# Gradient along rows: loads that wait for their slot's store only, and a second store in two pieces

## The chip, the cores and the metric

The kernel runs on one core of a Trainium2 chip. The metric is the time of one execution on the device, in microseconds (us); lower is better. A core has several engines with their own instruction streams. Three of them matter here: VectorE (DVE in the profile), which does the arithmetic; GpSimd (POOL), which does a little of it; and SyncE (SP), whose stream mostly issues transfers. ScalarE's stream (ACT) issues transfers too. Transfers between the main memory (HBM) and the on-chip memory (SBUF) run on sixteen DMA engines of the core. SP and ACT each have a queue of transfers on all sixteen; in the profile SP's is q1 and ACT's is q10.

## The reference

```python
def setup_inputs():
    return {"x": np.random.randn(8192, 8192).astype(np.float32)}

def reference(x):
    return np.gradient(x, axis=1)
```

Along each row, an inner element of the result is half the difference of its right and left neighbours: out[j] = (x[j+1] - x[j-1]) / 2. The first is x[1] - x[0], the last x[8191] - x[8190], both without the half. Input and output have 268.4 MB each, so 536.9 MB have to be moved.

## The kernel before, in words

The 8192 rows are cut into 32 tiles (`nsets`) of 256 rows. A tile gives each of the 128 partitions two neighbouring rows (`R = 2`), which lie side by side in HBM: 16,384 numbers, 64 KB a partition, 8.39 MB a tile. SBUF holds three slots (`NB = 3`) that the tiles use in turn. A slot is 64 numbers longer than a tile (`SH`): a tile is loaded 64 columns to the right, and its result is written from column 0, over the input that was already used. So a slot holds a tile from its load to the end of its store, and the load of tile i + 3 needs the store of tile i to be complete.

The order of the work is written out by hand (`manual_schedule`), and each instruction is told which earlier step it waits for (`chain`, L45 to L56; `keep` is the list of steps that it waits for). For tile i:

- SP issues the load (`load`, L60).
- GpSimd computes the four end differences of the two rows into `ends` (L72), as soon as the load has landed.
- VectorE computes the halved differences over both rows at once, 16,382 columns (L83). It also writes the two rows' ends wrongly, since it runs across the border between them.
- The right ends are copied over from `ends` (L94), by VectorE, or by GpSimd for tiles with i % 5 equal to 1 or 3.
- The store is issued (L97): by ACT for tiles 0 to 29, by SP for tiles 30 and 31.
- The load of tile i + 3 is issued by SP (L103, L60).

Tile 31 goes through L83, L94 and L97 twice, a row at a time, so the kernel has 33 stores; in this text stores 0 to 30 are those of tiles 0 to 30. Loads 0, 1 and 2 are issued at once at the start and stand behind each other in SP's queue.

From load 3 on a load waits for two things before it is issued: the store of tile i - 3 (L63), and the load in front of it, which must have landed (L62, `loads[-1]`, given the reason "queue empty"). SP works through its stream in order, so SP's queue never holds two loads after the first three.

Of the kernel before, what the change touches and what calls it, by code (L numbers as in the profile page):

```python
# [1 line left out]

# [4 lines left out]


@with_exitstack
def kernel(  # L10
    ctx: ExitStack,
    tc: tile.TileContext,
    x: bass.AP,
    out: bass.AP,
):

    nc = tc.nc
    P = nc.NUM_PARTITIONS
    n, m = x.shape
    R = 2
    NB = 3
    SH = 64  # L30
    W = R * m
    nsets = n // (P * R)
    f32 = x.dtype

    x_sets = x.rearrange("(s p t) m -> s p (t m)", p=P, t=R)
    out_sets = out.rearrange("(s p t) m -> s p (t m)", p=P, t=R)

    pool = ctx.enter_context(tc.tile_pool(name="pool", bufs=1))
    slots = [pool.tile([P, SH + W], f32, name=f"slot{k}", tag=f"slot{k}") for k in range(NB)]
    ends = pool.tile([P, nsets, R, 2], f32, name="ends", tag="ends")  # L40
    landed = mybir.DependencyInfo(mybir.DependencyClass.Sync, mybir.DependencyReason.DATA)
    loads, stores = [], [None] * nsets
    in_front = {}

    def chain(i, ins, *needed):  # L45

        group, engine = f"slot{i % NB}", ins.ins.engine
        keep = [o.ins for o in needed]  # L50
        if in_front.get(engine, (None,))[0] == group:
            keep.append(in_front[engine][1])
        tc.declare_no_dep(ins.ins, group=group, keep=keep, reason="implied by the needed step")
        tc.add_to_no_dep_group(group, ins.ins)
        in_front[engine] = group, ins.ins
        return ins  # L56

    def load(i):
        b = slots[i % NB]
        ins = nc.sync.dma_start(out=b[:, SH : SH + W], in_=x_sets[i])  # L60
        if i >= NB:
            tc.add_manual_dep(ins.ins, loads[-1].ins.name, landed, reason="queue empty")  # L62
        loads.append(chain(i, ins, *([stores[i - NB]] if i >= NB else [])))  # L63

    with tc.manual_schedule():
        for i in range(NB):
            load(i)
        for i in range(nsets):
            b = slots[i % NB]
            xin = b[:, SH : SH + W].rearrange("p (t m) -> p t m", m=m)  # L70

            ins = nc.gpsimd.tensor_sub(  # L72
                out=ends[:, i, :, :],
                in0=xin[:, :, 1 : m : m - 2],
                in1=xin[:, :, 0 : m - 1 : m - 2],
            )
            at = [chain(i, ins, loads[i])]
            last = i == nsets - 1
            nr = 1 if last else R
            for r in range(0, R, nr):  # L80
                c0, c1 = r * m + 1, (r + nr) * m - 1

                ins = nc.vector._custom_dve(  # L83
                    dve_ops.TENSOR_TENSOR_REDUCE_SUB_MAX,
                    out=b[:, c0:c1],
                    in0=b[:, SH + c0 + 1 : SH + c1 + 1],
                    in1=b[:, SH + c0 - 1 : SH + c1 - 1],
                    s0=0.0,
                    s1=0.5,
                )  # L90
                halved = chain(i, ins, *at)
                res = b[:, r * m : (r + nr) * m].rearrange("p (t m) -> p t m", m=m)
                placer = nc.gpsimd if i % 5 in (1, 3) and not last else nc.vector
                ins = placer.tensor_copy(out=res[:, :, 0 : m : m - 1], in_=ends[:, i, r : r + nr, :])  # L94
                placed = chain(i, ins, halved)
                queue = nc.scalar if i < nsets - 2 else nc.sync
                ins = queue.dma_start(  # L97
                    out=out_sets[i, :, r * m : (r + nr) * m], in_=b[:, r * m : (r + nr) * m]
                )
                stores[i] = chain(i, ins, placed)  # L100
                at = [halved]
            if i + NB < nsets:
                load(i + NB)  # L103


# [1 line left out]
_INS = ['x']  # L107
_OUTS = [((8192, 8192), 'float32')]


# [23 lines left out]
```

## Time and profile before

| | |
|---|---|
| time, median of 4 runs | 1248.5 us (1247.49 to 1319.02) |
| the profiled execution's time, its span | 1248.07 us, 1246.2 us |
| VectorE | 554.8 us busy, 45% of the span |
| GpSimd | 8.8 us busy |
| L83 over two rows | 17.22 us each, 31 times |
| issue of a load, of a store on ACT | 0.33 us, 0.34 us |
| a load, from issue to landing | 38.6 us (median) |
| a store on ACT, from issue to landing | 37.9 us (median) |

The four runs are 1248.07, 1248.93, 1247.49 and 1319.02 us. The span is the time from the first to the last instruction of the profiled execution. A row of the profile's groups names line, engine, operation and shape, then how often it ran, its busy time and the mean of one in ns, and the engine's idle time before it with what ended it. The chain is the sequence of steps that ended last, each followed back to what released it. In the DMA issues, "to landing" is the time from the issuing instruction to the completion of the transfer, so it includes the time that the transfer stood in its queue.

### The profile page before, as it was taken

The page shows a single profiled execution, that of the slowest core. Times are in us where ns is not written, and L with a number is a line of the kernel's source. Part 1 is how long each engine was busy: PE and PEld are TensorE (multiplying, and loading weights), DVE is VectorE, ACT ScalarE, POOL GpSimd, SP SyncE. Part 2 cuts the span into 40 slices and gives each one's busy share as a digit, 9 for nine tenths or more (in the row PEclk, how much of TensorE's full clock was granted, in tenths as well). Part 3 has the DMA queues.
Part 4 walks back from the last instruction along what each step waited for, and adds up shares of the span by engine and source line. Part 5 has one row for each costly group of instructions (what it writes and reads, how often), then busy time and mean ns, then how long its engine had stood idle before and what let it go on. Part 6 is the DMA issues. An engine that isn't in the chain of part 4 may idle for free.

```text
span 1246.2 us, 267 instructions
## 1 busy us (share of the span) xinstructions
DVE 554.8 (45%) x54; POOL 8.8 (1%) x48
## 2 busy tenths in 40 slices
DVE  2841453345533455334554245543355433554363
POOL 0000000000000000000000000000000000000000
DMA  9999999999999999999999999999999999999998
GB/s 404 438 438 438 423 429 427 435 433 438 438 435 438 438 429 431 427 433 433 435 438 433 435 438 412 433 431 433 431 433 438 431 417 431 438 438 433 438 438 374
DMA packets 9360, 536.88 MB, mean 431 GB/s; under 512 B 1040, under 2 KB 1040, under 8 KB 1040
## 3 DMA queue, kind: packets, MB, share of 16 engines
q1 hardware_dynamic: 5040, 285.21, 53.2%
q10 hardware_dynamic: 4320, 251.66, 46.6%
HBM read 268.44 MB, written 268.44 MB: 431 GB/s over the span
## 4 chain that ended last, share of the span: by engine, by line
DMA 93%; DVE 3%; issue 2%; SPq 0%; POOL 0%; POOLq 0%
DMA slot<-in_x_dram 90%; DMA out_dram<-slot 3%; DVE slot L83 3%; DVE slot L94 0%; SPq L60 0%; POOL ends L72 0%; POOLq L129 0%
## 5 line engine op out<-in xcount | busy, mean ns | idle before, releaser
L83 DVE CUSTOM_DVE_ANT_0 slot<-slot 128x16382 f32<-128x16382 f32 (+1 forms) x33 | 551.3, 16706 | 669.0 <-POOL ends L72 669.0
L72 POOL TENSOR_TENSOR ends<-slot 128x4 f32<-128x4 f32 x32 | 6.3, 198 | 989.9 <-DMA slot<-in_x_dram 989.9
L94 DVE COPY slot<-ends 128x4 f32<-128x4 f32 (+1 forms) x21 | 3.6, 171 | 0.7
L94 POOL COPY slot<-ends 128x4 f32<-128x4 f32 x12 | 2.3, 190 | 207.9 <-DVE slot L83 207.9
L118 POOL MEMSET const-uint8-127<- 128x1 uint8 x1 | 0.1, 102 | 0.0
L118 POOL MEMSET const-bfloat16-1.0<- 128x1 bf16 x1 | 0.1, 101 | 0.0
L118 POOL MEMSET const-float32-0.0<- 128x1 f32 x1 | 0.1, 98 | 0.2 <-issue 0.2
L118 POOL MEMSET const-float32-1.0<- 128x1 f32 x1 | 0.1, 99 | 0.0
## 6 DMA issues: line engine op xcount, KB each, us to landing
out_dram<-slot SPq DMA_DIRECT2D x2, 4096.0 KB, 20.3
slot<-in_x_dram SPq DMA_DIRECT2D x32, 38.6
out_dram<-slot ACTq DMA_DIRECT2D x30, 37.9
out_dram<-slot SPq DMA_DIRECT2D x1, 30.8
```

The lines of the kernel that those rows point to most:

```text
L72: ins = nc.gpsimd.tensor_sub(out=ends[:, i, :, :], in0=xin[:, :, 1 : m : m - 2], in1=xin[:, :, 0 : m - 1 : m - 2],)
L83: ins = nc.vector._custom_dve(dve_ops.TENSOR_TENSOR_REDUCE_SUB_MAX, out=b[:, c0:c1], in0=b[:, SH + c0 + 1 : SH + c1 + 1], in1=b[:, SH + c0 ...
L94: ins = placer.tensor_copy(out=res[:, :, 0 : m : m - 1], in_=ends[:, i, r : r + nr, :])
L118: nc = _bacc.Bacc("TRN2", target_bir_lowering=False, num_devices=1)
```

## The change

The load loses its wait for the load in front (L41 and L62 go). It waits for the stores of its slot alone, so a load may be issued while the one in front still runs, and then stands behind it in SP's queue. The list of stores of a tile becomes a list of lists, so that a load waits for each piece of the store. The store of tile 1 is issued as two transfers, one behind the other on ACT: the first 896 columns of the 16,384 (3,584 B a partition, 0.46 MB in all), and the other 15,488 (61,952 B a partition).

```diff
     W = R * m
+    FIRST = 896
     nsets = n // (P * R)
...
-    landed = mybir.DependencyInfo(mybir.DependencyClass.Sync, mybir.DependencyReason.DATA)
-    loads, stores = [], [None] * nsets
+    loads, stores = [], [[] for _ in range(nsets)]
...
         ins = nc.sync.dma_start(out=b[:, SH : SH + W], in_=x_sets[i])
-        if i >= NB:
-            tc.add_manual_dep(ins.ins, loads[-1].ins.name, landed, reason="queue empty")
-        loads.append(chain(i, ins, *([stores[i - NB]] if i >= NB else [])))
+        loads.append(chain(i, ins, *(stores[i - NB] if i >= NB else [])))
...
                 queue = nc.scalar if i < nsets - 2 else nc.sync
-                ins = queue.dma_start(
-                    out=out_sets[i, :, r * m : (r + nr) * m], in_=b[:, r * m : (r + nr) * m]
-                )
-                stores[i] = chain(i, ins, placed)
+                c0, c1 = r * m, (r + nr) * m
+                cuts = [c0, c0 + FIRST, c1] if i == 1 else [c0, c1]
+                for a0, a1 in zip(cuts, cuts[1:]):
+                    ins = queue.dma_start(out=out_sets[i, :, a0:a1], in_=b[:, a0:a1])
+                    stores[i].append(chain(i, ins, placed))
                 at = [halved]
```

## The prediction

> **What bounds the kernel now.** I read the page first (which engine is full), then the chain (what ends last), then the DMA queue's waits and issues, and last the times at which single tiles land.
>
> ```profile
> span 1246.2 us, 267 instructions
> DVE 554.8 (45%) x54; POOL 8.8 (1%) x48
> DMA packets 9360, 536.88 MB, mean 431 GB/s; under 512 B 1040, under 2 KB 1040, under 8 KB 1040
> q1 hardware_dynamic: 5040, 285.21, 53.2%
> q10 hardware_dynamic: 4320, 251.66, 46.6%
> DMA slot<-in_x_dram 90%; DMA out_dram<-slot 3%; DVE slot L83 3%; DVE slot L94 0%; SPq L60 0%; POOL ends L72 0%; POOLq L129 0%
> ```
>
> The queue rows give packet time as a share of sixteen DMA engines: 53.2% + 46.6% = 99.8%. The transfer engines are full from end to end; VectorE at 45% is not the bound. So removing a wait can't remove idle time. It can only alter how fast full engines work.
>
> ```profile
> 22.75 0.20 POOL L72 TENSOR_TENSOR ends<-slot 128x4 f32<-128x4 f32 x1 [22.31 <-DMA slot<-in_x_dram]
> 42.07 0.20 POOL L72 TENSOR_TENSOR ends<-slot 128x4 f32<-128x4 f32 x1 [19.12 <-DMA slot<-in_x_dram]
> 22.68:42.00 19.32, 17.39 (x2) 0.20 (x1) 1.00 1.00 434
> ```
>
> The timeline's first two rows are L72 starting as tiles 0 and 1 land; no store has begun, so the difference, 19.32 us, is what 8.39 MB costs alone, 434 GB/s in the windows' last column. All 64 tile-sized transfers at that rate take 64 x 19.32 = 1236.5 us. Before them lie 0.74 us to the first issue and 22.68 - 0.74 - 19.32 = 2.6 us until data flow; after the last landing (1245.31) 0.9 us. That makes 1240.7 us. The span has 5.5 us more: the whole of what can be won, 0.44%.
>
> ```profile
> SPq L60 <- DMA slot<-in_x_dram: 1162.0, 29, 77.0
> SPq L60 <- DMA out_dram<-slot: 2.4, 1, 2.4
> slot<-in_x_dram SPq DMA_DIRECT2D x32, 38.6
> out_dram<-slot ACTq DMA_DIRECT2D x30, 37.9
> ...
> 81.48 41.04 DMA slot<-in_x_dram
> 122.58 44.20 DMA slot<-in_x_dram
> 247.24 38.68 DMA slot<-in_x_dram
> 672.38 39.17 DMA slot<-in_x_dram
> 1021.67 39.71 DMA slot<-in_x_dram
> 1138.76 38.66 DMA slot<-in_x_dram
> ```
>
> SP's own waits: only load 3 was released by a store, all others by the load in front. The chain's rows (start, us) are loads end to end, each beside a store at half rate: 38.6 where two lone transfers would take 38.64. From 247.24 to 1177.48 (the 25 landings of tiles 6 to 30) the mean step is 930.24 / 24 = 38.76 us, 0.12 over the floor.
>
> **Where the 5.5 us sit.** The trace also holds every DMA packet. By start and end they fall into sixteen gapless rows, one per engine: 512 packets' worth each, one 64 KB packet 2.418 us, a 32 KB packet 1.213. Some packets are longer, nearly all of them loads. Per engine the excess is 0.7 us at the start and 0.8 us at 43.5 us (store 0 comes up), then 3.5 us on the mean engine and 5.0 on the slowest, which ends the kernel. Of the slowest's 5.0, 0.9 follow a load's issue by less than 8.2 us and 2.9 a store's issue; 1.0 fits neither. Those issues found their queue empty or nearly so. Where a transfer was queued well ahead (stores 1, 2 and 3, issued at 59.8, 96.8 and 140.3), the six microseconds after the issue show no long packet.
>
> **Part 1, the wait goes.** It removes 29 semaphore waits from SP and adds none; nothing is issued more often. Ahead of whom do loads move? On SP they stand in program order, stores 30 and 31 behind load 31, so no order changes there. ACT and POOL see nothing of it. How much earlier: in the steady part a store's issue follows the landing of its tile by 0.2 + 0.05 + 17.2 + 0.2 = 17.7 us and lands 37.9 later, at 55.6; two steps of 38.66 make 77.3; so the wait that is removed ends 21.7 us after its slot is free. But that lead grew while loads stalled. At the first place where the change bites, store 1 landed at 117.67 and load 3 at 122.52: load 4 comes 4.85 us earlier. From there both queues hold work, each engine alternates load and store packets, and nothing moves the lead again, so it stays near 5 us. Load 3 was issued at 81.48 and its first packet began at 85.36, 3.9 us later. A lead of 4.85 covers that, by about 1 us, for the engines that run last; for engines that run ahead by up to the 4.6 us spread of landings it doesn't. The last engines alone set the end.
>
> The load's time in the chain doesn't shrink: 38.6 us is two transfers at full rate. What goes is the excess at restarts. Lower end of the gain: 0, if the excess has another origin. Upper end: 5.0 us, all of the slowest engine's excess after 44 us. I take 0.9 + 2.9 = 3.8 us, because stores are then queued 20 us ahead too (store 2, issued 96.8, began about 117) and loads a little ahead, like the rows without excess.
>
> The cover: while load 4's queue stands empty, the store queue works alone. It stays that way in either version, so a late load costs no DMA time. If both queues were empty at once, the price would be the 3.9 us from issue to first packet for each tile; for that a store would have to be late by its 20 us of queueing, and VectorE has 21 us idle before each tile.
>
> **Part 2, store 1 in two pieces.** One more DMA issue on ACT (0.338 us by the row of L97), at 60 us, while store 0 runs to 81.47: hidden by 20 us. On the engines, 8 packets of 3,584 B and 8 of 61,952 replace 8 of 64 KB. The 32 KB packet costs 1.213 us, where half of 2.418 is 1.209: 4 ns per extra packet, 8 x 0.004 + one 9 ns completion packet = 0.04 us. Upper bound: the piece restarts a queue like store 0, 0.8 us. Below nothing: it puts load 3's first packet off by up to a packet and so gives loads more lead; that is at most the gain already counted. I take 0.1 us, near the 32 KB row, because the piece stands behind store 0 and ahead of the rest in a queue with work. The small packets take some 8 x 0.14 = 1.1 us from about 80.5, and load 3's packets come at about 85, so the two hardly meet; the phase shifts by under one packet. Load 4 now waits for two semaphores; both pieces land before load 3 does.
>
> The Trainium skill, "DMA: Bandwidth & Descriptors", section "Bandwidth", speaks against this: it asks for at least 1 MiB per DMA, and lists 0.95 us for 64 KB and 6.15 for 1 MB. The piece has 0.44 MiB; between those rows its estimate is 3.0 us, where its bytes at 434 GB/s are 1.06: by the page the part costs 2.0 us and the sum below would be 1246.3, no measurable change. The table is for transfers issued from GpSimd; no run here shows such a piece yet.
>
> **The tail** stays: 1206.58 to 1245.31 is 38.73 us for the two last tiles' stores, where two transfers need 38.64, with store 30 (30.8 us from issue) covering the last VectorE steps.
>
> **Sum.** The profiled execution took 1248.07 us, 1.9 over its span; the median shown is 1248.5 of four, one of them 70 us off, so I build on 1248.07. 1248.07 - 3.8 + 0.1 = 1244.4 us, 0.3% less. About 0.2%, 2.5 us, is what a measurement here can tell from no change.
>
> **Rivals.**
> *No change (1248).* The long packets belong to the mixing of reads and writes or to memory, not to restarts; or the change doesn't do what it says, since 1 us of spare lead is too thin and loads still find their queue dry. For it: DMA is full in both versions, and loads restarted at 300 to 560 us with hardly an excess (steps 38.64). Against: the clean queued transfers. Gain 0 to 2.5.
> *Slower (1261).* With both queues always full, every load packet runs between store packets; if the 39.17 us step of tile 17 to 18 became the rule, 28 steps would each cost 39.23 - 38.76 = 0.47 us more, +13 us; at the 39.71 us step it would be +28. It decides from 0.09 us per step (2.5 / 28). For it: slow steps exist and cluster (672 to 1061 us), so some alignments of the two streams hurt, and the change fixes an alignment that then never shifts. Against: from 46 to 78 and 86 to 114 us the streams alternated strictly, with every packet at 2.418 but for two, 0.02 and 0.07 us over.
> *Faster (1244.4)*, as summed.
>
> **How the numbers follow.** Faster as summed 0.46, no change 0.33, slower 0.21. The likeliest case's own range is 1242.9 (all 5.0 us, no cost of the piece: 1243.1, less 0.2 for spread of runs) to 1245.6. The overall range must hold no change (1245.6 to 1250.6) and the start of the slower case: 1242 to 1256. Below 1242 there is no room by the floor; what is left out is the upper part of the slower case.
>
> **What would show it.** Right: on SP, L60 waits for out_dram<-slot 28 or 29 times; issue to landing of loads grows from 38.6 to some 43 us, and of stores from 37.9 to some 58 (as store 1 and 2 now); loads still land every 38.64 us; DMA share stays at 99.8% and the span is 3 to 4 us shorter; packets grow by 144. Wrong: landings more than 38.85 us apart (slower); or 38.76 as now (no change). If a slice falls well below 431 GB/s with idle engines, the cover of the two queues failed, and the price is 3.9 us a time.

## The result and the profile after

The changed kernel is slower: median 1250.47 us against 1248.3, ratio 1.0028 with a 95% interval of 1.0018 to 1.0038. Forecast were 1244.4 us and a ratio of 0.997. Its single times lie further apart, from 1245.7 to 1258.0 us over 37 runs; its fastest is 0.5 us from the fastest of before (1245.2). The ratios in this text leave out executions more than 1.5% above the fastest of their kernel: 7 of the 164 of before (1305 to 1342 us), one of e1 (1337) and five of the six of e8 (1336 to 1343), and, between 1264 and 1284 us, three of the six of e9 and one each of e2, e3, e4, e12, e13, e15 and e16.

The page of the changed kernel, the rows that answer to those shown of before:

```profile
span 1250.9 us, 266 instructions
DVE 554.8 (44%) x54; POOL 8.8 (1%) x48
DMA packets 9504, 536.88 MB, mean 429 GB/s; under 512 B 1056, under 2 KB 1056, under 8 KB 1184
q1 hardware_dynamic: 5040, 285.21, 52.8%
q10 hardware_dynamic: 4464, 251.66, 46.4%
```

The two queues' packets take 52.8 + 46.4 = 99.2% of sixteen engines' span, where they took 99.8%. The work is the same; 0.8% of 1250.9 us, 10 us per engine, went unused, against 2.5 us before. The waits of SP and the DMA issues (issue to landing) show the change at work:

```profile
SPq L60 <- DMA out_dram<-slot: 1156.7, 29, 80.1
...
out_dram<-slot ACTq DMA_DIRECT2D x1, 7744.0 KB, 58.8
slot<-in_x_dram SPq DMA_DIRECT2D x32, 43.9
out_dram<-slot ACTq DMA_DIRECT2D x29, 54.9
out_dram<-slot ACTq DMA_DIRECT2D x1, 448.0 KB, 23.4
```

All 29 loads wait for a store now, none for a load. A load takes 43.9 us from issue to landing, that is 38.6 plus a stay of some 5 us in its queue. So the change does what it says. The time went elsewhere. The windows view of the last 19.9 us, before and then after (window, length, VectorE, GpSimd, clock, DMA share, GB/s):

```profile
1226.30:1246.20 19.90, 0.00 (x0) 0.00 (x0) 1.00 0.84 364
```

```profile
1231.00:1250.90 19.90, 0.00 (x0) 0.00 (x0) 1.00 0.52 226
```

At the end of the changed kernel half of the DMA time is empty. Each transfer reports its completion sixteen times, once for each engine; of the last store's sixteen reports, after the first, thirteen lie within 0.12 us, two at 1.3 and 1.4, and one at 8.84 us. In the kernel before fourteen lie within 0.7 us and the last two at 2.0 and 2.1. So one engine is late. An estimate from these reports: without it the profiled execution would have ended 8.84 - 1.42 = 7.4 us earlier, at 1253.08 - 7.4 = 1245.7 us, which is what the fastest runs take. The profiled execution is 2.6 us above the median, and there is no trace of a median one; so that a late engine also makes the 2.2 us between the medians fits, but is not shown.

That engine falls behind slowly. The time between the first and last report of a store grows like this (us):

| store of tile | 5 | 10 | 15 | 20 | 25 | 29 |
|---|---|---|---|---|---|---|
| before | 4.6 | 4.5 | 4.6 | 4.2 | 1.5 | 4.3 |
| after | 3.3 | 6.7 | 7.5 | 11.6 | 13.8 | 17.1 |

(A report comes after the packet of the other queue that is in between, so part of a spread is the turn at which an engine changes queue; the growth is the late engine's.) The long packets tell the same. Over 2.418 us for each 64 KB, the mean engine loses 3.5 us after 44 us in the kernel before and 0.9 after. Followed by start and end, the sixteen rows of before lose 4.4 to 6.7 us in all, startup included; those of after 1.3 to 4.3, and one about 9. Summed up along these rows, the late engine of after has done 1.5 us less work than the median engine at 400 us, 3.4 at 800 and 7.0 at 1200; in before, at steps of 50 us up to 1200, no engine is ever more than 1.9 us behind, and none stays there to the end.

### The profile page after: what moved, and what is told of

The parts are those of the page before. It is cut to its first block, busy times and chain, and to the rows that moved or that the text cites. A ratio compares the mean times of both kernels' runs of the same rounds, so it can differ in the third digit from the quotient of the medians.

```text
span 1250.9 us, 266 instructions
## 1 busy us (share of the span) xinstructions
DVE 554.8 (44%) x54; POOL 8.8 (1%) x48
## 3 DMA queue, kind: packets, MB, share of 16 engines
q1 hardware_dynamic: 5040, 285.21, 52.8%
q10 hardware_dynamic: 4464, 251.66, 46.4%
## 4 chain that ended last, share of the span: by engine, by line
another core or an unknown queue 83%; DMA 9%; issue 3%; DVE 3%; SPq 1%; POOL 0%; POOLq 0%
DMA slot<-in_x_dram 5%; DMA out_dram<-slot 3%; DVE slot L81 3%; SPq L60 1%; DVE slot L92 0%; POOL ends L70 0%; POOLq L131 0%
## 6 DMA issues: line engine op xcount, KB each, us to landing
out_dram<-slot SPq DMA_DIRECT2D x2, 4096.0 KB, 20.3
slot<-in_x_dram SPq DMA_DIRECT2D x32, 43.9
out_dram<-slot ACTq DMA_DIRECT2D x29, 54.9
```

## The experiments

The table comes first, and what each run tells follows. "Excess" is what the mean engine loses in long packets after 44 us, "last" how far the engine that ends last lies behind the one before it; both are of one profiled execution. "Step" is the share of load packets in whose middle fewer than 12 of the other 15 engines load, that is, packets that are out of step with the rest.

| kernel | ratio to before (95%) | excess us | last us | step |
|---|---|---|---|---|
| before | 1 | 3.5 | 0.1 | 18% |
| after | 1.0028 (1.0018 to 1.0038) | 0.9 | 7.4 | 10% |
| e1 second part alone | 1.0008 (0.9998 to 1.0018) | 4.3 | 0.1 | 28% |
| e2 first part alone | 1.0026 (0.9998 to 1.0055) | 5.7 | 8.7 | 22% |
| e3 both parts again | 1.0014 (0.9996 to 1.0031) | 0.9 | 6.0 | 15% |
| e4 both, halves | 1.0051 (1.0019 to 1.0084) | 6.0 | 8.6 | 25% |
| e5 one queue | 1.0022 (1.0012 to 1.0032) | 3.4 | 0.1 | |
| e7 no wait, one engine late | 1.0068 (1.0046 to 1.0090) | 3.6 | 8.7 | 24% |
| e8 wait, one engine late | none | 8.2 | 0.1 | 17% |
| e9 wait at every 2nd load | 1.0075 (1.0056 to 1.0094) | 12.7 | 0.5 | 40% |
| e10 wait at every 8th | 1.0129 (1.0112 to 1.0146) | 10.8 | 0.0 | 46% |
| e11 load 3 in four | 1.0161 (1.0141 to 1.0181) | 20.3 | 0.2 | 84% |
| e12 load 3 in two | 1.0159 (1.0115 to 1.0203) | 19.4 | 2.1 | 63% |
| e13 one tiny load | 1.0113 (1.0076 to 1.0149) | 7.2 | 4.4 | 16% |
| e14 two tiny loads | 1.0099 (1.0085 to 1.0112) | 7.6 | 2.7 | 20% |
| e15 both parts, one tiny load | 1.0076 (1.0051 to 1.0101) | | | |
| e16 half of the engines shifted | 1.0032 (1.0008 to 1.0055) | 7.9 | 0.8 | 81% |

**Which part is it (e1 to e4).** The theory: without the wait one engine collects what is lost (straggler). Rivals: the piece costs, or the lead of the loads decides.

```diff
# e1: the changed kernel, and the wait back
+        if i >= NB:
+            tc.add_manual_dep(ins.ins, loads[-1].ins.name, landed, reason="queue empty")
# e2: the changed kernel without the piece
-                cuts = [c0, c0 + FIRST, c1] if i == 1 else [c0, c1]
+                cuts = [c0, c1]
# e4: the changed kernel
-    FIRST = 896
+    FIRST = 8192
```

> The second part alone: loads keep their wait for the load in front, the store of tile 1 goes in two pieces. Straggler theory (without the wait one DMA engine collects the long packets and ends the kernel alone): ratio to before 1.000, within 0.001, last landings of the engines 2 to 3 us apart. Piece theory (the piece costs): ratio 1.002 to 1.004.

> The first part alone: no wait for the load in front, the store of tile 1 in one piece. Straggler theory: ratio 1.002 or more, single times spread over 1246 to 1258 us, the last landings of the engines 5 us or more apart. Piece theory: ratio 1.000 or below.

> Both parts, the changed kernel as it is, beside the two parts alone. Both theories: ratio 1.002 to 1.004. Straggler theory: in a profile that is faster than the one shown, the last landings are closer together, and in a slower one farther apart, by as much as the time differs; the mean engine's excess stays near 2.3 us in each.

> As the changed kernel, the first piece 8192 columns in place of 896. Straggler theory: the piece only shifts the two queues against each other at tile 1, which decides nothing about the wait, so ratio 1.001 to 1.008 like without a piece. Alignment theory (the lead of the loads, fixed at tile 1, sets the time): a clearly different ratio from the kernel with 896 columns, by 0.003 or more, with a lead that differs by some packets in the profile.

The piece alone gives 1.0008, its interval with 1 just inside: a cost of about 1 us, at most 2.2, with single times from 1246.5 to 1254.2. The missing wait alone gives 1.0026, the changed kernel again 1.0014, both with 1 inside the interval, because single times run from 1245.4 to some 1260 us. So the width, not the median, is what tells the parts apart: it comes with the missing wait and not with the piece. The windows view of the last 19.9 us, of the piece alone and of the missing wait alone:

```profile
1227.00:1246.90 19.90, 0.00 (x0) 0.00 (x0) 1.00 0.85 367
```

```profile
1238.90:1258.80 19.90, 0.00 (x0) 0.00 (x0) 1.00 0.52 222
```

With the wait the engines end together (0.85), without it half of the DMA time is empty (0.52), in a profile of 1258.8 us span. In that one fifteen engines reported the last store within 0.2 us and one 8.7 later. The last report comes 8.7 to 8.9 us after the first in after, e2, e3, e4, e7 and e13 alike. In part that is the tail's doing: the last stores are issued as VectorE gets through tile 31, which the late engine's part of the load holds up, so the others stand idle at 1221 to 1226 us, 3 to 4 us each in e2 and up to 0.9 in after. In e3 they do not stand idle, and the 8.7 us are the late engine's own.

e3's expectation that the mean excess stays at 2.3 us in startup and run together holds (0.9 after 44 us, as in after). In e2 the excess is larger than in after because the others lose too: from 750 us on, some 75 first packets of stores are long, by 0.55 us in the mean. By then each store is issued 6 to 10 us after the first engines have reported the store in front, so their queue of stores has run dry, for want of tiles that the late engine holds up; that engine is 9.2 to 9.8 us behind the median one from 500 us to the end and falls no further back.

e4's lead (by how much a load is issued before the one in front has landed) was 9.6 to 10.3 us from load 9 on, as e2's, against 5 in after and e3; the ratio of e4 is higher than e3's by 0.0037, as the alignment theory asked, and within the straggler theory's range too, and the intervals meet. Whether the 896 columns help the kernel without a wait stays open.

**A late engine made on purpose (e7, e8), one queue (e5), loads alone (e6).** The theory by now: load packets are long where the other engines store, so an engine out of step loses more (mixing).

```diff
# e7: e2, and e8: the kernel before, both with one more load in front
+    odd = pool.tile([17, 1024], f32, name="odd", tag="odd")
     with tc.manual_schedule():
+        nc.sync.dma_start(out=odd[:, :], in_=x[0:17, 0:1024])
# e5: e2 with all transfers in SP's queue
-                queue = nc.scalar if i < nsets - 2 else nc.sync
+                queue = nc.sync
-            if i + NB < nsets:
-                load(i + NB)
+            if 1 <= i < nsets - 2:
+                load(i + 2)
# e6: e2 without the stores of tiles 0 to 28
+                if i < nsets - NB:
+                    stores[i] = placed
...
```

> As the first part alone (no wait, no piece), with one more load ahead of all: 17 rows of 4 KB into a tile of its own, 68 KB, which one DMA engine alone should carry, so that it starts some 2.6 us behind the others. Mixing theory: the engine that is out of step from the start loses more at each tile, so the long times become the rule: median 1256 us or more, ratio 1.006 or more, last landings 8 us apart. Chance theory (stragglers come and go by chance and a delay adds only itself): the time of the first part alone plus 2.6 us, ratio 1.003 to 1.005.

> The kernel before with the same extra load of 68 KB on one engine. Mixing theory with a wait that sets the engines in step again: at most 2.6 us more than before, ratio 1.000 to 1.002. If the wait does not hold the engines together: ratio 1.005 or more, like without the wait.

e7's times came out as the mixing theory said: median 1256.24 us, ratio 1.0068, the fastest run 1252.68. The extra load put one engine some 3 us behind at tile 0 (first to last report of load 0: 3.11 us in e7, 2.75 in e8, 0.54 in before). At the store of tile 5 of e7 the spread was 19.4 us, and it stayed at 21 to 22 to the end. e8 has no ratio, so its expected ratio wasn't put to the test, and whether the extra load itself makes long executions common is open. The profiles alone can be compared (that of e8 took 1253.3 us): with the wait the spread of the stores goes down again.

| store of tile | 5 | 10 | 15 | 20 | 25 | 29 |
|---|---|---|---|---|---|---|
| e7, no wait | 19.4 | 21.1 | 21.1 | 21.4 | 22.2 | 21.7 |
| e8, wait | 15.3 | 13.8 | 9.9 | 9.4 | 4.9 | 4.9 |

The work done tells the same. Behind the median engine, the late one of e7 is 6.8 us at 100 us, 8.7 at 600 and 8.7 at 1000; that of e8 is 4.7 and 2.8, and at 1000 us no engine is more than 0.9. So most of the loss came in the first 100 us, before the wait differs, and not a little more at each tile as the mixing theory had it; after that the wait brings the late engine back, and without the wait it stays behind.

But the wait does not win time: the mean engine of e8 lost 8.2 us, of e7 3.6. With the wait the engines in front lose until the late one is level; without it the late one stays behind. The windows of the last 19.9 us of e7 have the same 0.52:

```profile
1235.20:1255.10 19.90, 0.00 (x0) 0.00 (x0) 1.00 0.52 222
```

> The stores of tiles 0 to 28 are left out, so that part of the output is not written; loads wait for VectorE's last step on their slot. Mixing theory: no load packet over 2.6 us between the first microseconds and load 31, loads land every 19.32 us with the engines within 1 us. Restart theory: each of 29 loads brings some long packets, as in the kernel before (5 or more a load).

Loads alone lose nothing. The windows view of e6 over loads 1 to 29:

```profile
22.68:600.00 577.32, 518.26 (x47) 8.21 (x42) 1.00 1.00 433
```

433 GB/s through 577 us, and from 44 to 600 us no packet over by more than 0.12 us. When the first of the stores came beside the last load, one engine lost 3.4 us in eleven long packets within 37 us. So in these runs long packets come with stores beside the loads.

> No wait for the load in front and no piece; all loads and stores stand in SP's one queue in the order store i, load i + 2, so that an engine does the 8 packets of a store and then the 8 of a load, in place of a load packet and a store packet in turn. Mixing theory (a load packet is slowed while the other engines store, so an engine that has fallen out of step loses more): few packets overlap with the other kind, so the mean excess after 44 us falls below 0.5 us, the last landings lie within 2 us, ratio 0.994 to 0.998. Restart theory (the excess belongs to a transfer that starts): the same number of starts, mean excess stays at 1 us or more, ratio 0.998 to 1.003.

e5's ratio of 1.0022 is the restart theory's, not that of mixing. Its twelve times lie closer together than those of after (1248.2 to 1252.4), and its rows lose 3.4 us, most of it in the last packet of a load, where the engine goes over to a store (over 140 of 158 long packets after 44 us). So taking load and store in turn isn't the whole cause: long packets also stand at the change from one to the other.

**Some waits (e9, e10).** If the wait levels the engines, a wait now and then might keep the small excess and lose the late engine.

```diff
-        if i >= NB:
+        if i >= NB and i % 2 == 0:      # e9; e10: i % 8 == 0
             tc.add_manual_dep(ins.ins, loads[-1].ins.name, landed, reason="queue empty")
```

> The kernel before with the wait for the load in front on every second load only (even tiles from 4 on). Straggler theory, as the runs so far have it (the wait makes the other engines take the excess, so that the late one comes back): a wait at every second load still holds the engines together, ratio 0.998 to 1.001, last landings within 3 us, mean excess between 0.9 (no wait) and 4.3 us (wait at each load). Rival (only an unbroken row of waits does it): ratio 1.002 to 1.005, single times over 1253 us.

> The same wait on tiles 8, 16 and 24 only. Straggler theory: between two waits a late engine can lose 0.5 us a tile, 4 us in all, and three waits bring back little of it, so ratio 1.001 to 1.004 and the engine that ends last 4 us or more behind the others. Rival (a few waits are enough to set the engines in step): ratio 0.996 to 0.999, mean excess below 2 us, last landings within 3 us.

Both theories failed on the time. e9 is at 1.0075 (the median of all six times, 1267.9 us, would be 1.6% over), e10 at 1.0129, worse than the wait always or never. The late engine isn't the reason in e9 (last landings 0.5 us apart between the last two); the mean excess is, 12.7 and 10.8 us. In e10 the spread of the loads is 3.3 us at load 8, the first that waits, 13.8 at load 15, and stays near 19 from load 20 on; two engines end 4.8 us behind the others. The table's last column shows what the two have more of: 40 and 46% of load packets out of step. In before, after and e1 to e10 (e5 and e6 aside), load packets in step lost some 2 to 31 ns each after 44 us, those out of step 17 to 114, more in every single run. That is a relation, not yet a cause.

**More lead (e11 to e15).** In after a load comes 5 us ahead of need and takes 4 us from issue to its first packet. If that is too thin, more lead should end the excess.

```diff
# e11: e2, load 3 as four transfers of 32 partitions; e12: two of 64
+        step = P // 4 if i == NB else P
+        loads.append([])
+        for p0 in range(0, P, step):
+            ins = nc.sync.dma_start(
+                out=b[p0 : p0 + step, SH : SH + W], in_=x_sets[i, p0 : p0 + step]
+            )
+            loads[i].append(chain(i, ins, *(stores[i - NB] if i >= NB else [])))
...
# e13: e2, e15: the changed kernel, with one tiny load behind load 3; e14: e2 with two (range(2))
...
+        if i == NB:
+            for k in range(1):
+                nc.sync.dma_start(out=turns[:, k, :], in_=x[0:16, k * 128 : (k + 1) * 128])
```

> No wait for the load in front, no piece of store 1; in its place load 3 goes as four transfers of 32 partitions each, one behind the other. The packets stay at 64 KB; only three completions more stand in SP's queue, each of which gives a store packet a turn, so that the stores get ahead by up to three packets, 7 us. Margin theory (engines fall out of step where the next load comes too late for some of them: the lead of 5 us, less 4 us from issue to first packet, is under their spread): lead about 12 us, fewer load packets out of step than the 9 to 22% of the runs without a wait, mean excess under 0.9 us, last landings within 3 us, ratio 0.995 to 0.998. Chance theory (an engine that is late for any cause collects the excess, whatever the lead): ratio 1.001 to 1.005, single times from 1245 to 1260 us as in the first part alone.

> The same with load 3 as two transfers of 64 partitions: one more completion, the stores ahead by up to one packet more, a lead of some 7.5 us. Margin theory: between the first part alone and the four pieces, ratio 0.997 to 1.001. Chance theory: ratio 1.001 to 1.005.

> The first part alone (no wait, no piece), and behind load 3 one tiny load of 16 rows of 512 B into a tile of its own: one packet and one completion on each engine, two turns of SP's queue, in which the stores get two packets, 4.8 us, ahead for the rest of the run. Thin lead as the cause: lead 10 us, no long packets after the first tiles, engines end within 2 us, ratio 0.994 to 0.998, single times within 3 us of each other. Late engine as the cause: lead 10 us, but single times from 1245 to 1265 us and ratio 1.001 to 1.006.

> The same with two tiny loads, four turns: lead some 15 us, and the stores wait only 6 us in their queue. Thin lead as the cause: like one tiny load if 6 us are enough for stores (0.994 to 0.999), else long packets return at the start of stores. Late engine as the cause: 1.001 to 1.006.

> The changed kernel (no wait, 896 columns first) with the one tiny load behind load 3. Thin lead as the cause: as with the tiny load alone, ratio 0.994 to 0.998, so that the piece is worth nothing by itself. Late engine as the cause: ratio 1.001 to 1.004 as the changed kernel.

By ratio e11 and e12 are the slowest of all. The windows view of e11 shows where (the last column is GB/s):

```profile
82.00:150.00 68.00, 15.40 (x2) 0.00 (x0) 1.00 1.00 324
150.00:250.00 100.00, 52.01 (x5) 0.78 (x4) 1.00 1.00 419
250.00:650.00 400.00, 173.36 (x17) 2.94 (x15) 1.00 1.00 435
650.00:1050.00 400.00, 186.89 (x17) 2.74 (x14) 1.00 1.00 434
```

While the four transfers ran, loads and stores together moved 324 GB/s: load packets took 4.55 us (median from 82 to 120 us) in place of 2.418. After 250 us, though, nothing was lost: 2,816 load packets up to 1100 us, none long, with a lead of 9.7 us, and the spread of the stores unchanged at 4.7 us from tile to tile. This is the state I was after, but the 20 us that the mean engine lost all came before it.

That lead is no more than e2 has without the four transfers, 9.6 us or more from load 9 on. The issues of e2 and then of e11 (issue to landing) show it:

```profile
slot<-in_x_dram SPq DMA_DIRECT2D x32, 48.8
```

```profile
slot<-in_x_dram SPq DMA_DIRECT2D x35, 48.3
```

So e11 did not add lead, and its quiet state is not owed to lead: e2 with the same lead lost 5.7 us and had a late engine. e13 and e14 did add lead (14 to 15 us in their traces from load 7 on), and it did not help: 1.0113 and 1.0099, e15 1.0076. So a thin lead is not the cause. In e13 the spread of the loads grew from 3 us at tile 5 to 18.5 at tile 15 in spite of it. Rather, more lead went with more excess: 0.9 us at a lead of 5 (after, e3; e7 3.6), some 6 at 9.7 (e2, e4), over 7 at 14.5 (e13, e14), with the quiet state of e11 as the exception. That too is a relation only.

**Half of the engines shifted (e16).** In e11 after 300 us, 7 to 9 engines were loading for 73% of the time; in after 0 to 2 or 14 to 16 for three quarters of it. Perhaps an even mixture is what keeps packets short.

```diff
# e2, with a load of two 512 B pieces in each of 8 rows behind load 3
...
+        if i == NB:
+            two = x[0:8].rearrange("p (a c) -> p a c", a=2)
+            nc.sync.dma_start(out=turns[:, :, :], in_=two[:, :, 0:128])
```

> The first part alone (no wait, no piece), and behind load 3 a tiny load of 8 rows of two 512 B pieces, which eight engines should carry with two packets and a completion each: three turns of SP's queue on these eight, so that from then on eight engines load while the other eight store. Balance as the cause (packets are long where 15 engines store and one loads): 7 to 9 engines loading at any time, mean excess after 150 us below 0.5 us, engines end within 2 us, ratio 0.995 to 0.998. If a late engine loses in any mixture: ratio 1.002 or more, and the excess per engine over 2 us.

The shift took place: from 130 to 160 us exactly 8 engines were loading for 57% of the time. Yet the mean engine lost 0.3 to 0.8 us in most 50 us stretches up to 750 us, 7.9 in all, and the ratio is 1.0032. The balance theory falls. What remained of it: the loss was spread over the engines (the last ones 0.8 us apart), and the state drifted apart again (7 to 9 engines loading for some 25% of the time after 830 us), which e11's did not.

No kernel tried beats the one before.

## Why the prediction was wrong

- *DMA is full, and the 5.5 us above the floor are the whole of what can be won.* Nothing speaks against it: no time of a kernel with all its stores is under 1245 us. It bounded the gain, not the loss.
- *The wait goes: 29 waits, no order changes, loads come some 5 us ahead and nothing moves that lead.* So it came out: each load from 4 to 31 was issued 4.8 to 5.3 us before the one in front landed. Issue to landing came out at 43.9 for loads (43 forecast) and 54.9 for stores (58). But there is luck in it: in e2, the first part alone, the lead was 6.5 us at load 4 and grew to 9.8, so something does move it.
- *The excess at restarts goes.* Right in the mean of after and e3: 3.5 to 0.9 us after 44 us. In e2 the mean is 5.7, of which 75 x 0.55 / 16 = 2.6 us are first packets of stores that found their queue dry. The stretches that I cited as clean follow the issue of stores 1 to 3, when these still stood in the queue (store 2 began about 117), so they could not show that a queued transfer starts without excess. And the three parts of the slowest engine's 5.0 add up to 4.8 only; the part that fits neither is 1.2 us.
- *"I take 0.9 + 2.9 = 3.8 us", the excess of the slowest engine.* This is the step that failed. It gave the engine that ends last the relief that the mean one had: 5.0 - 3.8 = 1.2 us should have been left to it after 44 us, and it lost 7.2 in after. The engines are coupled through the slots: a tile is ready when the last engine has it. Of the excess that is left (0.9 x 16 = 14.4 us over all engines) half fell, from 200 us on, on a single engine; it lost some 7 us more than most others. I had written that the last engines alone set the end, and not asked what keeps them level. In before the wait does: the losses are spread over all sixteen rows, 4.4 to 6.7 us, and e8's late engine comes back where e7's does not. It is not the only way to stay level: e11 and e16 have no wait and no late engine.
- *Part 2 costs 0.1 us.* The packets cost what I worked out: 8 x 0.140 + 8 x 2.286 = 19.41 us against 8 x 2.418 = 19.34, so 0.07 us. The Trainium skill, "DMA: Bandwidth & Descriptors", section "Bandwidth", would by an estimate from its table give the piece 3.0 us; this run shows 8 x 0.140 = 1.12. Whether the piece costs anything through the alignment is not settled (1.0008, interval to 1.0018). That it gives loads more lead did not come true: the lead is 5 us with it (after, e3) and 9.7 without (e2).
- *The tail stays.* In length yes: from the landing of load 31 (1211.27) to the last store (1249.99) 38.72 us, as before 38.73. The 4.7 us more were there at the landing of load 31, 1206.58 before.
- *Slower, 1261.* The sign and the threshold held: the mean step from tile 6 to 30 is (1175.04 - 240.99) / 24 = 38.92 us, over the 38.85 that I had named. The mechanism was not mine: not every load packet pays, one engine does.

What stays open is what makes a single load packet long. Shown is that it came only with stores beside it (e6), that load packets out of step with the other engines lose more in every run up to e10 where the two can be told apart (a relation, not shown to be the cause, and not so in e11 and e12, where the loads in pieces lost most of all), that neither a thin lead (e13, e14) nor an uneven mixture (e16) explains it, and that a state without any exists (e11 after 250 us, at the lead that e2 has). Why that state holds and the one of e16 does not, I can't say.

## What to carry to other kernels

When DMA is full, ask what keeps the sixteen engines level: a wait that looks idle on the queue may be what spreads small losses over all of them, and the kernel ends with the worst engine, not with the mean. Look at the DMA share in the last slice of the span and at the first and last report of a transfer; a growing distance is a late engine. Try such a wait at every transfer and at none, and not only now and then: in this kernel the wait at some loads (e9, e10) cost 0.75% or more and 1.3%.

## What the runs showed of the hardware

- A transfer's completion takes a turn of its queue like a data packet. In e13 the tiny load behind load 3 was reported by the first engine at 126.80 us, load 3 itself at 121.94: 4.86 us, two packets of the other queue, one for the tiny packet and one for its completion. The Trainium skill, "DMA: Bandwidth & Descriptors", section "Queues, rings and completion order", has the engines go round the queues packet by packet; here a turn was one 64 KB run or one completion.
- While load 3 went in transfers of 32 or 64 of the 128 partitions, beside stores, a 64 KB load packet took some 4.6 us (median from 82 to 120 us, 4.55 in e11 and 4.60 in e12), and 2.418 us in the same stretch with all 128 (e2).
- With loads alone the engines stayed at 433 GB/s for 577 us, with hardly a long packet (e6); in these runs, what is lost beyond the rate of one transfer comes with stores beside loads.
